# Stick-breaking attention in chunks of at most 512 keys, as one continuous pipeline, with the kept fractions left in PSUM

## The chip, the cores and the metric

The kernel runs on one core of a Trainium2 chip. The metric is the device time of one execution in microseconds. The profile names the engines PE (TensorE, matrix products; PEld is its weight loads), DVE (VectorE), ACT (ScalarE), POOL (GpSimd) and SP (SyncE, which issues most DMAs). Each engine works through its own instructions in a fixed order and waits at an instruction whose inputs or buffers are not ready.

## The reference

One decoder layer on 1024 tokens of 1024 channels. After a first norm and an input projection, two attention families run side by side (NSA, and stick-breaking); they are projected up, merged by gates, projected out, and a squared-ReLU channel mixer follows. The change touches stick-breaking attention alone: 8 heads of 64 channels, strictly causal, with a running product over keys in place of a softmax.

```python
z = jnp.einsum('bqhd,bshd->bhqs', qb, k).astype(jnp.float32) * scale
mask = key_pos[None, :] < t[:, None]
log_keep = jnp.where(mask, jax.nn.log_sigmoid(-z), 0.0)
suffix = lax.cumsum(log_keep, axis=3, reverse=True) - log_keep
a = jnp.where(mask, jnp.exp(jax.nn.log_sigmoid(z) + suffix), 0.0)
return jnp.einsum('bhqs,bshd->bqhd', a.astype(v.dtype), v)
```

So the weight of key s for query t is sigmoid(z) at s times the product of sigmoid(-z), the kept fractions, over all keys between s and t.

## The kernel before

The kernel takes its stages one after another: norm and projections, NSA attention, stick-breaking attention, up projections and merge, output projection, channel mixer. While the two attention stages run, a side stream of matrix products fills TensorE: `fill_all` computes 28 column blocks of the input projection, 48 products of 512 columns each (line 739, tiles `pd`). `drive` (lines 1027 to 1036) steps through the attention's generator; each step yields a nominal cost, and `drive` then issues fill products until their nominal 0.216 us each have used up `cost * ratio + extra`. For stick-breaking the ratio is 0.6 and the extra 0.1, and the last 96 products are kept back for the time after the stage.

A head's queries and keys are loaded from a DRAM buffer and split into a high and a low part (`prep`: a cast on ScalarE, three instructions on GpSimd); values are turned and split for two heads at a time (`prep_v`). The stage then takes 16 families, the lower four row tiles (`g` = 0, rows 0 to 3 of 128 queries) and the upper four (`g` = 1, rows 4 to 7) of each head.

`sb_a` does the first half of a family. Row tile i has n = 128 (i + 1) keys. Its scores come in one PSUM bank (tile `psx`, three buffers), or in two when n is over 512, by products with Kh and Kl and one that adds the causal mask (lines 1109 to 1112). ScalarE turns each bank into the kept fractions, `keep` in SBUF, and into `sig` in SBUF (lines 1113, 1114). One score bank later, `fin` runs for the whole row of n keys: VectorE scans `keep` from its last key to its first into the running product `Pt` (line 1122; its second input is a broadcast zero, in SBUF too), and GpSimd multiplies `sig` by it (line 1124).

`sb_b` does the second half, one family later, interleaved with the next `sb_a`. Key tile n goes upwards from 0: up to four 128x128 pieces of `sig` are transposed into one bank `pt` (line 1140, two buffers); ScalarE casts it to `th`, VectorE subtracts for `tl` (lines 1153, 1154, three buffers each); two products with the values add them to the one bank `po` (line 1145). When the last key tile is in, ScalarE copies half of the bank out (line 1161), VectorE adds the other half (`osum`, line 1163), and SP stores the sum. The next family's first product into `po` must wait for that read.

All instructions of one engine stand in the order of a planner; a dependency set by `behind` keeps fill products behind the attention products they were traced after.

Of the kernel before, what the change touches and what calls it, by code (L numbers as in the profile page):

```python
# [6 lines left out]
F32 = mybir.dt.float32  # L7
# [8 lines left out]
S = 1024  # L16
# [19 lines left out]
def build(tc, I, out):  # L36
# [31 lines left out]
    def rsqrt(dst, ssum, n, tmp):  # L68
        """dst = (ssum / n + eps) ** -0.5, one Newton step behind the table's root; tmp: two more tiles"""
# [36 lines left out]
    # ---------------------------------------------------------------- constants  # L106
# [23 lines left out]
    # ---------------------------------------------------------------- x and the modulation  # L130
    def mod_cols():
# [11 lines left out]
        # (1 + b) g of the first scale  # L143
# [94 lines left out]
    def split_w1(raw, n, m=0):  # L238
        """columns of one contraction tile; the last m of them in tiles of their own"""
# [13 lines left out]
    # query rows: norm, gain and 1/8, then transposed to DRAM  # L253
# [23 lines left out]
    # with the contraction outermost: both compression inputs (transposed) and three tiles of queries  # L277
# [36 lines left out]
    # the first half of the tokens goes ahead for two contraction tiles  # L314
# [92 lines left out]
    # later modulation rows (gate1, shift2, scale2, gate2): partial sums, kept for the end  # L407
# [47 lines left out]
    # relative-position bias: one row per distance, then Toeplitz tiles through DRAM  # L455
# [12 lines left out]
    def bias_cmp():  # L468
# [4 lines left out]
        # row 127 - p holds what distance 128 + p - x asks for; the exchange matrix turns the rows round  # L473
# [11 lines left out]
    # compressed blocks: two positions of one head to a contraction  # L485
# [14 lines left out]
    def compress(which):  # L500
# [9 lines left out]
        def add(g, hs=(0, 1)):  # L510
            # rows r * 64 + d, block c, pair of positions j: src[d, 16 c + 8 g + 2 j + r] + pos[8 g + 2 j + r, d]
# [65 lines left out]
    # selected and window keys and values, and the branch gates  # L577
# [65 lines left out]
    done = [("q", t, qb[t]) for t in range(3)]   # products that wait for their elementwise part  # L643
    turn = []                                   # those that wait for their transposes
# [51 lines left out]
    # column blocks of the input projection, transposed: out[cols, t]  # L696
# [23 lines left out]
    def track(ins):  # L720
        """the attention's latest instruction on the tensor engine"""
        last[:] = [ins.ins]

    def behind(ins):
        """the filling products keep behind the attention's instructions they were traced after"""
# [24 lines left out]
    # ---------------------------------------------------------------- NSA attention  # L750
# [10 lines left out]
    # and the strictly causal one of a diagonal block  # L761
# [36 lines left out]
    # scores, row maxima and exponentials of two heads; the weights end up scaled by gate over sum  # L798
    def nsa_a(i, kv, hp, qT, P):
# [41 lines left out]
        # compressed blocks  # L841
# [15 lines left out]
        # the chunks of a row share its maximum  # L857
# [21 lines left out]
    # transposed weights times values: rows 0-63 of the result carry V's high part, 64-127 its low part  # L879
# [76 lines left out]
    def interleave(ga, na, gb, nb_, lead):  # L956
        """steps of ga with steps of gb spread over those after the first `lead`"""
# [69 lines left out]
    def drive(main, fill, ratio, extra=0.0, keep=0):  # L1027
        """fill beside the main work, all but the last `keep` products of it"""
# [9 lines left out]
    def pump(fill, us):  # L1038
        """that much of it without waiting for anything"""
# [8 lines left out]
    # ---------------------------------------------------------------- stick-breaking attention  # L1048
    def sb_gens(sp):
# [14 lines left out]
        def prep(h, ld):  # L1064
            """split the head's operands, one engine instruction or two per step"""
# [31 lines left out]
        def sb_a(g, ops, A):  # L1097
            Q, Kh, Kl = ops
            late = []
            for i in range(4 * g, 4 * g + 4):  # L1100
                n = 128 * (i + 1)
                keep = sp.tile([128, S], F32, name="keep", bufs=2)
                sig = sp.tile([128, 512 * (g + 1)], F32, name="sig%d" % g, bufs=4)
                A[i] = sig
                for c0, c1 in ([(0, n)] if n <= 512 else [(n - 512, n), (0, n - 512)]):
                    p = psx()
                    w = c1 - c0
                    qs = Q[:, i * 128:(i + 1) * 128]
                    track(nc.tensor.matmul(p[:, :w], qs, Kh[:, c0:c1], start=True, stop=False))
                    track(nc.tensor.matmul(p[:, :w], qs, Kl[:, c0:c1], start=False, stop=c1 != n))  # L1110
                    if c1 == n:
                        track(nc.tensor.matmul(p[:, w - 128:w], identr, diagr, start=False, stop=True))
                    nc.scalar.activation(keep[:, c0:c1], p[:, :w], AF.Sigmoid, scale=-(HD ** -0.5))  # L1113
                    nc.scalar.activation(sig[:, c0:c1], p[:, :w], AF.Sigmoid, scale=HD ** -0.5)  # L1114
                    if late:
                        late.pop(0)()
# [441 lines left out]
```

## Time and profile before

| | us |
|---|---|
| three timed runs | 1803.51, 1809.74, 1809.12 |
| median | 1809.12 |
| span of the profiled execution | 1806.0 |
| stick-breaking stage in it, from the first transposes of values (631.2) to its last product (901.5) | 270.3 |

The profile is of one execution; its times count from the start of its span. An instruction's row has its start, its duration and its engine. Busy time is the union of an engine's instructions. A matrix product's row is longer than the distance to the next one, because products overlap in the array.

### The profile page before, as it was taken

How to read it: one execution, taken by the hardware profiler on the slowest of the kernel's cores; microseconds unless marked ns; L12 is line 12 of the kernel's file. 1: busy time of each engine (PE TensorE's matmuls, PEld its weight loads, DVE VectorE, ACT ScalarE, POOL GpSimd, SP SyncE). 2: the span in 40 equal slices, each digit the busy share in tenths (PEclk: the TensorE clock that was granted, in tenths of full speed). 3: DMA queues.
4: the chain of work that ended last, by engine and by line, in shares of the span. 5: the costliest groups of instructions: out<-in, count | busy, mean ns of one | idle time of the engine just before them, and what ended most of it. 6: DMA issues, size and time to landing. Idle time of an engine off the chain costs nothing.

```text
span 1806.0 us, 25077 instructions
## 1 busy us (share of the span) xinstructions
PE 1705.9 (94%) x8620; PEld 1418.7 (79%) x8620; DVE 1181.2 (65%) x2459; ACT 784.9 (43%) x1745; POOL 1004.8 (56%) x889
## 2 busy tenths in 40 slices
PE   5888999999999979888799999999999999999998
PEld 4768889888888867677678788688888888888886
DVE  7797578778777486767744466256556565657458
ACT  5423376666666355545532234333333333333332
POOL 5463243444333476745338434487677685868576
PEclk9999999999999999989899999999999999999999
DMA  9355412112111342321086462311111121202012
GB/s 298 86 153 170 114 48 60 53 52 61 46 53 41 110 115 76 97 74 36 24 272 191 153 203 59 116 40 55 47 58 59 35 66 40 70 24 71 25 34 93
DMA packets 151047, 157.15 MB, mean 87 GB/s; under 512 B 13240, under 2 KB 112776, under 8 KB 150920
## 3 DMA queue, kind: packets, MB, share of 16 engines
q1 hardware_dynamic: 146696, 153.45, 28.4%
q10 hardware_dynamic: 4224, 2.10, 0.4%
q8 instruction: 68, 1.11, 0.3%
q14 instruction: 59, 0.48, 0.1%
HBM read 128.24 MB, written 27.28 MB: 86 GB/s over the span
## 4 chain that ended last, share of the span: by engine, by line
PE 73%; DVE 9%; POOL 6%; issue 5%; DMA 4%; ACT 2%; SPq 0%; POOLq 0%; ACTq 0%; DVEq 0%
PE px L1457 20%; PE px L1506 16%; PE pd L739 14%; PE px L1370 5%; PE po L902 4%; PE pt L936 3%; DVE Pt L1122 2%; PE psx L818 2%; PE psx L819 2%; PE po L1145 2%; DMA adraw<-in_ada_w_dram 1%; PE pt L1140 1%; POOL adacc L441 1%; PE cb L298 1%; POOL wh L63 1%
## 5 line engine op out<-in xcount | busy, mean ns | idle before, releaser
L1509 DVE TENSOR_TENSOR acc<-acc,px 128x512 f32<-128x512 f32 x384 | 243.8, 681 | 122.5 <-PE px L1506 116.7
L1457 PE MATMUL px<-mtl,wh 128*128 128x512 f32 x512 | 205.0, 400 | 0.0
L1457 PE MATMUL px<-mth,wh 128*128 128x512 f32 x512 | 202.1, 395 | 0.0
L1457 PE MATMUL px<-mth,wl 128*128 128x512 f32 x512 | 201.2, 393 | 0.0
L739 PE MATMUL pd<-uh,uwh 128*128 128x512 f32 x448 | 183.2, 409 | 0.7 <-ACT zo L1011 0.7
L739 PE MATMUL pd<-ul,uwh 128*128 128x512 f32 x448 | 178.7, 399 | 0.0
L66 DVE TENSOR_TENSOR wl<-raw,wh 128x1024 fp32r<-128x1024 f32 x48 | 74.6, 1553 | 159.1 <-ACT wh L61 133.9
L739 PE MATMUL pd<-uh,uwl 128*128 128x512 f32 x448 | 178.2, 398 | 0.0
L1506 PE MATMUL px<-wbl,rah 128*128 128x512 f32 x448 | 175.7, 392 | 2.1 <-POOL wbl L1482 1.8
L1506 PE MATMUL px<-wbh,ral 128*128 128x512 f32 x448 | 174.7, 390 | 0.0
L1506 PE MATMUL px<-wbh,rah 128*128 128x512 f32 x448 | 172.8, 391 | 0.0
L1482 POOL TENSOR_TENSOR wbl<-raw,wbh 128x1024 fp32r<-128x1024 f32 x40 | 104.0, 2600 | 92.3 <-ACT wbh L1481 92.1
L1124 POOL TENSOR_TENSOR sig<-sig,Pt 128x128 f32<-128x128 f32 (+3 forms) x64 | 100.5, 1578 | 83.0 <-ACT sig L1114 42.8
L894 DVE TENSOR_TENSOR tl<-pt,th 128x512 fp32r<-128x512 f32 (+8 forms) x168 | 103.6, 619 | 34.2 <-ACT th L893 33.4
L1480 POOL TENSOR_TENSOR raw<-r 128x512 f32<-128x512 f32 x80 | 109.9, 1394 | 21.1 <-DVE wl L66 19.0
L1122 DVE TENSOR_TENSOR_SCAN Pt<-keep,zero 128x128 f32<-128x128 f32 (+3 forms) x64 | 109.3, 1726 | 13.9 <-ACT keep L1113 3.7
L1457 PEld LDWEIGHTS px<-mth,wh 128*128 128x128 f32 x512 | 96.3, 188 | 24.5 <-issue 0.2
L893 ACT CAST th<-pt 128x512 fp32r<-128x512 f32 (+8 forms) x168 | 88.6, 530 | 61.4 <-PE pt L936 58.8
L1457 PEld LDWEIGHTS px<-mth,wl 128*128 128x128 f32 x512 | 96.3, 188 | 23.8 <-issue 0.8
L1457 PEld LDWEIGHTS px<-mtl,wh 128*128 128x128 f32 x512 | 96.4, 188 | 22.8 <-DVE ral L1489 0.5
L1481 ACT CAST rah<-raw 128x1024 fp32r<-128x1024 f32 x40 | 42.0, 1050 | 153.8 <-PE px L1506 140.5
L875 POOL TENSOR_TENSOR pcx<-pcx,tot 128x64 f32<-128x64 f32 (+7 forms) x32 | 10.5, 330 | 172.0 <-DVE tot L873 82.6
(326 smaller groups left out, 4706.4 us busy)
## 6 DMA issues: line engine op xcount, KB each, us to landing
adraw<-in_ada_w_dram SPq DMA_DIRECT2D x64, 256.0 KB, 2.9
raw<-in_mlp_w_dram SPq DMA_DIRECT2D x32, 512.0 KB, 4.2
w<-in_mlp_w_dram SPq DMA_DIRECT2D x32, 512.0 KB, 3.5
z_d<-zo SPq DMA_DIRECT2D x56, 256.0 KB, 2.1
uwr<-in_w_in_dram SPq DMA_DIRECT2D x54, 256.0 KB, 3.1
xa<-in_ada_w_dram SPq DMA_DIRECT2D x32, 256.0 KB, 5.8
zr<-z_d SPq DMA_DIRECT2D x32, 256.0 KB, 4.0
m<-z_d SPq DMA_DIRECT2D x32, 256.0 KB, 3.6
```

Of the source, the lines that this page charges most:

```text
L66: (nc.vector if e == "v" else nc.gpsimd).tensor_tensor(dst, src, f(h), op=OP.subtract)
L739: r = nc.tensor.matmul(p, a, b, start=(k == 0 and n == 0), stop=(k == NK - 1 and n == 2))
L893: nc.scalar.copy(th[:rows, :w], p[:rows, :w])
L894: nc.vector.tensor_tensor(tl[:rows, :w], p[:rows, :w], f(th)[:rows, :w], op=OP.subtract)
L1122: nc.vector.tensor_tensor_scan(Pt[:, 0:n][:, ::-1], keep[:, 0:n][:, ::-1], zero.to_broadcast([128, n]), 1.0, op0=OP.mult, op1=OP.add)
L1124: nc.gpsimd.tensor_tensor(sig[:, :n], sig[:, :n], Pt[:, 1:n + 1], op=OP.mult)
L1370: nc.tensor.matmul(p, a[:, k, ts_], b[:, k % 2], start=(k == 0 and n == 0), stop=(k == NK - 1 and n == 2))
L1457: nc.tensor.matmul(p, a[:, k], b[th][:, k], start=(k == 0 and m == 0), stop=(k == NK - 1 and m == 2))
L1480: nc.gpsimd.tensor_tensor(d, block(i0, j0, s), block(i1, j1, s), op=OP.add if sg > 0 else OP.subtract)
L1482: (nc.vector if e == "v" else nc.gpsimd).tensor_tensor(l.rearrange("p s n -> p (s n)"), src, f(h).rearrange("p s n -> p (s n)"), op=OP.sub ...
L1506: nc.tensor.matmul(p, a[:, s, qs], b[:, s], start=(s == 0 and n == 0), stop=(s == 1 and n == 2))
L1509: nc.vector.tensor_tensor(acc[:, t, ds_], acc[:, t, ds_], p, op=OP.add if sg > 0 else OP.subtract)
```

## The change

Only `sb_a`, `sb_b` and `sb_all` are rewritten, and one call of `drive`; the rest of the diff removes comments and is left out here.

- The work of a head is now in three kinds of groups of four chunks each. Kind 0: rows 3 to 0, all their keys. Kind 1: rows 7 to 4, the last 512 keys of each. Kind 2: rows 7 to 4, the keys before these (512, 384, 256, 128). The chunks have the widths that the score banks had before, but each chunk now has a scan and a multiplication of its own: 96 scans for 64. A chunk of kind 2 starts its scan from the last value of the row's chunk of kind 1, which a one-column copy on VectorE brings next to it.
- The kept fractions are written by ScalarE back into the score bank (`p`, in PSUM), after `sig` and not before it, and the scan reads them there. The tile `keep` is gone. The bank is held until the scan is done.
- Rows and key tiles go downwards. One step does one chunk's scores and sigmoids, the scan and multiplication of the chunk before, the transposes of one key tile of the group before, the products with values of tiles split earlier, and the split of the tile turned a step before. `bank`, `turned` and `split_` carry tiles over from family to family.
- A family's first products with values are put off by one step (`wait`). Its first product covers only the columns of one row tile; the rest of the bank is written by later ones.
- `th` and `tl` have four buffers, `Pt` six of 513 columns, `sig` five or two.
- The ratio of `drive` is 0.55 and its extra 0.08.

```diff
-        def sb_a(g, ops, A):
...
-                    nc.scalar.activation(keep[:, c0:c1], p[:, :w], AF.Sigmoid, scale=-(HD ** -0.5))
-                    nc.scalar.activation(sig[:, c0:c1], p[:, :w], AF.Sigmoid, scale=HD ** -0.5)
...
-                    nc.vector.memset(Pt[:, n:n + 1], 1.0)
-                    nc.vector.tensor_tensor_scan(Pt[:, 0:n][:, ::-1], keep[:, 0:n][:, ::-1],
-                                                 zero.to_broadcast([128, n]), 1.0, op0=OP.mult, op1=OP.add)
-                    nc.gpsimd.tensor_tensor(sig[:, :n], sig[:, :n], Pt[:, 1:n + 1], op=OP.mult)
...
+        def chunks_of(kind):
+            rows = range(3, -1, -1) if kind == 0 else range(7, 3, -1)
+            out_ = []
+            for i in rows:
+                n = 128 * (i + 1)
+                out_.append((i,) + ((0, n), (n - 512, n), (0, n - 512))[kind])
+            return out_
+
+        def sb_a(kind, chunk, ops, A, edges):
...
+            sig = sp.tile([128, w], F32, name="sigr" if kind == 1 else "sig%d" % w, bufs=5 if kind == 1 else 2)
+            nc.scalar.activation(sig, p[:, :w], AF.Sigmoid, scale=HD ** -0.5)
+            nc.scalar.activation(p[:, :w], p[:, :w], AF.Sigmoid, scale=-(HD ** -0.5))
+            A[i, kind] = (sig, c0)
+
+            def fin():
+                Pt = sp.tile([128, 513], F32, name="Pt", bufs=6)
+                if diag:
+                    nc.vector.memset(Pt[:, w:w + 1], 1.0)
+                else:
+                    nc.vector.tensor_copy(Pt[:, w:w + 1], edges.pop(i)[:, 0:1])
+                nc.vector.tensor_tensor_scan(Pt[:, 0:w][:, ::-1], p[:, 0:w][:, ::-1], zero.to_broadcast([128, w]),
+                                             1.0 if diag else Pt[:, w:w + 1], op0=OP.mult, op1=OP.add)
+                nc.gpsimd.tensor_tensor(sig, sig, Pt[:, 1:w + 1], op=OP.mult)
+                if kind == 1:
+                    edges[i] = Pt
...
+                for c in range(4):
+                    cost = 0.0
+                    if k < len(groups):
+                        fin, cost = sb_a(kind, chunks[c], ops[h], A[h, min(kind, 1)], edges)
+                        late.append(fin)
+                        yield cost
+                    if len(late) > 1 or k == len(groups):
+                        if late:
+                            late.pop(0)()
+                    cost = 0.0
+                    if k > 0:
+                        hb, kb = groups[k - 1]
+                        g = min(kb, 1)
+                        cost += turn(hb, g, (3, 7, 3)[kb] - c, A[hb, g])
+
+                        if split_ and (wait[0] or split_[0][2] != 4 * split_[0][1] + 3):
+                            while len(split_) > 0:
+                                cost += times_v(V)
+                            wait[0] = 0
+                        elif split_:
+                            wait[0] = 1
+                        if len(turned) > 1:
+                            halves()
+                    yield cost
...
-    drive(sb_gens(sp), fill, 0.6, 0.1, TAIL)
+    drive(sb_gens(sp), fill, 0.55, 0.08, TAIL)
```

`turn` holds the transposes of one key tile, `halves` the cast and the subtraction, `times_v` the two products with values and, after key tile 0, the read of the bank; each is the old code of `sb_b` with its tiles taken from the lists.

## Rows read from the trace of the kernel before

**Rows 1.** The page: span, and busy time, share of the span and instructions of each engine.

```profile
span 1806.0 us, 25077 instructions
PE 1705.9 (94%) x8620; PEld 1418.7 (79%) x8620; DVE 1181.2 (65%) x2459; ACT 784.9 (43%) x1745; POOL 1004.8 (56%) x889
```

**Rows 2.** Busy time by stretch: the whole stage, the part of it in which fill products run, the last whole piece of that part, and the part without them. Columns: from and to, length, busy time and instructions of PE, PEld, DVE, ACT and POOL, granted clock, DMA share, GB/s.

```profile
631.20:901.50 270.30, 229.43 (x1173) 188.09 (x1172) 195.26 (x279) 147.36 (x336) 161.98 (x103) 0.92 0.26 71
...
631.20:866.30 235.10, 203.79 (x1048) 168.08 (x1047) 170.91 (x244) 128.82 (x297) 151.57 (x96) 0.95 0.29 79
...
832.00:866.30 34.30, 31.66 (x171) 26.48 (x170) 24.99 (x41) 18.70 (x45) 17.95 (x14) 1.00 0.10 32
866.30:901.50 35.20, 25.64 (x126) 20.01 (x125) 24.35 (x36) 18.54 (x40) 10.42 (x7) 0.76 0.07 19
```

**Rows 3.** Timeline of PE in a piece without a wait: start, duration, instruction, and how many stand together.

```profile
847.27 0.39 PE L739 MATMUL pd<-uh,uwh 128*128 128x512 f32 x1
847.50 0.39 PE L1145 MATMUL po<-th,V 128*128 128x512 f32 x1
...
848.43 0.60 PE L1140 MATMUL pt<-ident,sig 128*128 128x128 f32 x4
848.78 0.48 PE L1145 MATMUL po<-tl,V 128*128 128x512 f32 x1
849.10 0.39 PE L739 MATMUL pd<-ul,uwh 128*128 128x512 f32 x1
```

**Rows 4.** Groups of instructions on PE in the stage, 631.2 to 901.5 (one of three groups of fill products, the transposes, one of two groups of products with values, one of two of scores): count, then busy time and mean ns, then idle time before them and its releasers.

```profile
L739 PE MATMUL pd<-uh,uwh 128*128 128x512 f32 x135 | 57.1, 423 | 0.0
L1140 PE MATMUL pt<-ident,sig 128*128 128x128 f32 x288 | 53.3, 295 | 25.7 <-DVE tl L1154 14.5 <-DVE V L1092 5.5 <-POOL sig L1124 3.5
L1145 PE MATMUL po<-tl,V 128*128 128x512 f32 (+1 forms) x96 | 41.3, 431 | 6.2 <-DVE tl L1154 6.2
...
L1109 PE MATMUL psx<-Kh,Q 128*128 128x512 f32 (+2 forms) x96 | 34.7, 365 | 1.3 <-ACT sig L1114 1.3
```

**Rows 5.** The same groups in the last whole piece with fill products (832 to 866.3; one of three), and the line of the fill products from 631.2 to 866.3 with the first and last start of this group.

```profile
L739 PE MATMUL pd<-uh,uwh 128*128 128x512 f32 x24 | 9.7, 403 | 0.0
...
L739 PE MATMUL pd<-uh,uwl x135: 387/393/628, 631.8 to 865.8; 128*128 128x512 f32 x135
```

**Rows 6.** Who waited for whom, the weight loads of PE in the stage: us in total, times, longest.

```profile
PEld pt L1140 <- DVE tl L1154: 20.0, 17, 4.3
PEld po L1145 <- DVE tl L1154: 7.1, 5, 2.4
PEld pt L1140 <- POOL sig L1124: 5.9, 4, 2.0
PEld po L1145 <- DVE osum L1163: 5.6, 7, 1.9
...
PEld psx L1109 <- ACT sig L1114: 1.5, 1, 1.5
```

**Rows 7.** Timeline of DVE: four scans, 128 columns twice, 512 and 1024 once, and a low part of a fill weight, both of whose inputs lie in SBUF.

```profile
658.36 2.56 DVE L1122 TENSOR_TENSOR_SCAN Pt<-keep,zero 128x128 f32<-128x128 f32 x1 [1.29 <-ACT sig L1114]
...
675.01 0.69 DVE L66 TENSOR_TENSOR uwl<-uwr,uwh 128x512 fp32r<-128x512 f32 x1
...
790.60 2.27 DVE L1122 TENSOR_TENSOR_SCAN Pt<-keep,zero 128x1024 f32<-128x1024 f32 x1
...
836.29 1.21 DVE L1122 TENSOR_TENSOR_SCAN Pt<-keep,zero 128x512 f32<-128x512 f32 x1
...
860.63 0.40 DVE L1122 TENSOR_TENSOR_SCAN Pt<-keep,zero 128x128 f32<-128x128 f32 x1
```

**Rows 8.** Timeline of POOL: the low part of a head's keys, and multiplications of 128 and 512 columns.

```profile
658.28 2.35 POOL L66 TENSOR_TENSOR Kl<-zr,Kh 128x1024 fp32r<-128x1024 f32 x1
...
763.35 0.41 POOL L1124 TENSOR_TENSOR sig<-sig,Pt 128x128 f32<-128x128 f32 x1
...
867.20 1.09 POOL L1124 TENSOR_TENSOR sig<-sig,Pt 128x512 f32<-128x512 f32 x1 [1.25 <-DVE Pt L1122]
```

**Rows 9.** The lines of the scan and of the subtraction `tl` in the stage: count, then minimum, median and maximum duration in ns.

```profile
L1122 DVE TENSOR_TENSOR_SCAN Pt<-keep,zero x64: 401/1694/3833, 635.4 to 885.4; 128x128 f32<-128x128 f32 x8, 128x256 f32<-128x256 f32 x8, 128x384 f32<-128x384 f32 x8, 128x512 f32<-128x512 f32 x8
...
L1154 DVE TENSOR_TENSOR tl<-pt,th x96: 258/608/693, 650.1 to 901.0; 128x512 fp32r<-128x512 f32 x48, 128x384 fp32r<-128x384 f32 x16, 128x256 fp32r<-128x256 f32 x16, 128x128 fp32r<-128x128 f32 x16
```

**Rows 10.** Groups of instructions of DVE and POOL in the stage, columns as in the groups of PE.

```profile
L1122 DVE TENSOR_TENSOR_SCAN Pt<-keep,zero 128x128 f32<-128x128 f32 (+3 forms) x64 | 109.3, 1726 | 13.9 <-ACT keep L1113 3.7 <-issue 3.6 <-ACT sig L1114 2.9
L1154 DVE TENSOR_TENSOR tl<-pt,th 128x512 fp32r<-128x512 f32 (+1 forms) x96 | 51.4, 546 | 37.1 <-ACT th L1153 35.0 <-ACT sig L1114 1.6
L66 DVE TENSOR_TENSOR uwl<-uwr,uwh 128x512 fp32r<-128x512 f32 x18 | 20.1, 1139 | 4.6 <-POOL uwh L63 4.6
...
L1121 DVE MEMSET Pt<- 128x1 f32 x62 | 3.7, 59 | 7.9 <-POOL sig L1124 7.0 <-PE pt L1140 0.8
...
L1124 POOL TENSOR_TENSOR sig<-sig,Pt 128x128 f32<-128x128 f32 (+3 forms) x64 | 100.5, 1578 | 83.0 <-ACT sig L1114 42.8 <-DVE Pt L1122 19.2 <-DVE Pt L1121 13.6
```

**Rows 11.** Groups of instructions of ACT in the stage: kept fractions, `sig` and the cast `th`.

```profile
L1113 ACT ACTIVATE keep<-psx 128x512 f32<-128x512 f32 (+2 forms) x96 | 47.9, 508 | 50.6 <-DVE Pt L1122 24.8 <-PE psx L1112 10.2 <-DVE Pt L1121 8.1
L1114 ACT ACTIVATE sig<-psx 128x512 f32<-128x512 f32 (+2 forms) x96 | 47.7, 511 | 18.9 <-PE pt L1140 17.9 <-POOL Q L1073 0.7
L1153 ACT CAST th<-pt 128x512 fp32r<-128x512 f32 (+1 forms) x96 | 46.7, 492 | 34.4 <-PE pt L1140 33.7
```

More of the change, by code (lines that the diff above doesn't have):

```diff
@@ new lines, in sb_gens, with turn @@
+        bank, turned, split_, wait = {}, [], [], [0]
+        def turn(h, g, kt, A):
+            p = pt()
+            c0 = max(0, kt - 4 * g) * 128
+            for i in range(max(4 * g, kt), 4 * g + 4):
+                o = (i - 4 * g) * 128
+                sig, s0 = [A[i, x] for x in ((0,) if g == 0 else (1, 2)) if (i, x) in A and
+                           A[i, x][1] <= kt * 128 < A[i, x][1] + A[i, x][0].shape[1]][0]
+                track(nc.tensor.transpose(p[:, o:o + 128], sig[:, kt * 128 - s0:kt * 128 - s0 + 128], ident))
+            turned.append((h, g, kt, c0, p))
+            return (512 - c0) / 128. * PT_
@@ new lines, in sb_all @@
+            groups = [(h, kind) for h in range(8) for kind in range(3)]
+            A, edges, late = {}, {}, []
+            extra = []
+            for k in range(len(groups) + 1):
+                if k < len(groups):
+                    h, kind = groups[k]
+                    if kind == 0:
+                        A[h, 0] = {}
+                        if h + 1 < 8:
+                            lds[h + 1] = (load((h + 1) // 2, h + 1), load(4 + (h + 1) // 2, h + 1))
+                            if h % 2 == 1:
+                                vr = load_v((h + 1) // 2)
+                    if kind == 1:
+                        A[h, 1] = {}
+                        if h + 1 < 8:
+                            extra.append(prep(h + 1, lds[h + 1]))
+                            if h % 2 == 1:
+                                extra.append(prep_v(vr, V))
+                    chunks = chunks_of(kind)
+                for c in range(4):
+                    cost = 0.0
+                    if k < len(groups):
+                        fin, cost = sb_a(kind, chunks[c], ops[h], A[h, min(kind, 1)], edges)
[18 more added lines that the diff above has]
+                    yield cost
+                    for e in list(extra):
+                        r = next(e, "end")
+                        if r == "end":
+                            extra.remove(e)
+                        elif isinstance(r, tuple):
+                            ops[h + 1] = r
+                        elif r:
+                            yield r
+                if k < len(groups) and kind == 2:
@@ L1205, in sb_all @@
                                 ops[h + 1] = r
-                    prev = (h, g, V[h], A)
-            for c in sb_b(*prev):
-                yield c
+                            elif r:
+                                yield r
+                    extra = []
+            while turned or split_:
+                cost = 0.0
+                while split_:
+                    cost += times_v(V)
+                if turned:
+                    halves()
+                yield cost
         return sb_all()
```

118 lines of the change are left out of this document (33 added, 85 removed).

## The prediction

> **What bounds the kernel now.** I read the page first [rows 1]: TensorE is busy for 94% of the span, so only stretches in which it has holes can give anything back. The change touches one stage, so I cut that stage out by time [rows 2]: it runs from 631.2 to 901.5, 270.3 us, and here TensorE is busy for 229.4 us, VectorE for 195.3, GpSimd for 162.0 and ScalarE for 147.4. No engine is full. The reader should also see the granted clock: 1.00 in the piece from 832 to 866.3, 0.92 over the stage, 0.76 in the last piece. Where TensorE has holes its clock falls between its two levels, 1.2 and 2.4 GHz, and that costs time again.
>
> Busy time flatters TensorE, since its rows overlap, so I counted its work by distances between starts [rows 3]. A product of 512 columns takes 0.23 us (847.27 to 847.50). Four transposes and one such product take 0.67 (848.43 to 849.10), so a transpose takes (0.67 - 0.23) / 4 = 0.11. A mask product of 128 columns I count as a quarter of 0.23, 0.06. The stage has [rows 4] 3 x 135 = 405 fill products (93.2 us); scores and products with values of 8 heads, 18432 columns a head or 36 x 0.23 (66.2); 64 masks (3.7); 288 transposes of weights and 32 of values (35.2). That is 198.3 us, 73% of the stage; 72 us are holes and slow clock. The 768 instructions that are no fill take 105.1 us, 0.137 each.
>
> Where are the 72 us? The last fill product before the end starts at 865.8 [rows 5]. Behind it 126 instructions [rows 2], 17.3 us of work, take 35.2: 49%, 17.9 us lost. Ahead of it 181.0 us of work take 235.1: 77%, 54.1 us lost. The best piece, 832 to 866.3, has 3 x 24 fill products [rows 5] and 99 others, 16.6 + 13.6 = 30.1 us in 34.3: 88%. The waits name what TensorE's weight loads stand for [rows 6]: `tl` with 20.0 and 7.1 us, the multiplied `sig` with 5.9, the read of the one bank `po` with 5.6. So the stage is bound by what VectorE and GpSimd hand back late, and at its end by a lack of fill.
>
> Why is `tl` late? Its own length isn't the reason, 693 ns at most [rows 9]. It stands in VectorE's queue behind scans, and these are long: 401 ns at least, 3833 at most. A scan of 128 columns takes 0.40 us once and 2.56 another time [rows 7]; the long one starts at 658.36 and ends at 660.92, and beside it GpSimd works from 658.28 to 660.63 [rows 8]. The scan stood for the whole of that instruction. Both of its inputs lie in SBUF. `tl`, which has one of its two in PSUM, never stretches.
>
> **The change part by part.**
>
> *The scan reads PSUM.* Undisturbed scans take 0.40, 1.21 and 2.27 us for 128, 512 and 1024 columns [rows 7], 2.09 ns a column, so the eight lengths of a head take 10.7 us and the stage 85.6. They took 109.3 [rows 10]: 23.7 us, 0.37 a scan, are waits for GpSimd. After, a head has six scans of 512 and two each of 384, 256 and 128: 7.26 + 2 x (0.94 + 0.67 + 0.40) = 11.28 us, the stage 90.2. I take it that a scan with one input in PSUM waits for GpSimd as little as `tl` does. Then VectorE has 195.3 - 109.3 + 90.2 = 176.2 us. Multiplications gain likewise: 0.41 and 1.09 us for 128 and 512 columns alone [rows 8], or 0.18 + 1.77 ns a column, give 82.6 us for the 96 against 100.5 now [rows 10]; GpSimd goes to 144.
>
> What does a PSUM input cost by itself? `tl` of 512 columns takes up to 0.69 us with one input in PSUM [rows 9]; a subtraction of the same size with both in SBUF takes 0.69 alone [rows 7]. So nothing, and the sum goes by that. A rule speaks against it: the Trainium skill, Perfetto Trace Analysis, section Optimizing Scalar/DVE Operations, gives VectorE about 60 ns of access time on SBUF and about 125 on PSUM. By it 96 scans would cost some 6 us more on VectorE (an estimate from that page), and the forecast would be 1774 at most; the rows show no such difference.
>
> *The copies.* 32 one-column copies: 0.059 each if they are like the one-column memset [rows 10], 1.9 us; at most 1.09 each, if each waits for a multiplication of 512 [rows 8], 35 us. I take 1.9, since the memset is the nearest in size; VectorE has 178 us.
>
> *ScalarE writes into PSUM.* No row of before shows that. The kept fractions take 47.9 us now [rows 11]. If reading and writing one bank took turns they would take twice that, and ScalarE 195 us in place of 147; if it is cheaper than SBUF, the gain falls on an engine that is idle for 45% of the stage. I take 0, as `sig` and the kept fractions, same reads, cost the same; the upper end stays in the range.
>
> *The bank is held for the scan.* Cost on the path: none with three banks, since one chunk's products, two sigmoids and scan take 0.5 + 1.0 + 1.2 us [rows 3, 7, 11] against three steps of 228.6 / 96 = 2.4. Behind a score product that waits stand all transposes, products with values and fill. What if that cover fails is a rival below.
>
> *Downwards, a step at a time.* Each transposed piece is now multiplied three steps ahead of its use, for row 7 as for row 4. The waits for `sig` (5.9) and, through `wait`, for `po` (5.6) go; the longest instruction ahead of a `tl` in VectorE's queue is 1.2 us, no longer 2.3 to 3.8. What is late next is `tl` itself, behind ScalarE's `sig`, kept fractions and `th` of the same step. `th`, `tl`, loads, head splits and stores are as many as before; they cost nothing new. The fourth buffers and the reversed accumulation cost nothing either.
>
> *The fill.* By the code the generator yields 250 times before, 132.3 us of nominal cost; (132.3 x 0.6 + 250 x 0.1) / 0.216 = 483 products wanted, and 404 are to be had (the trace has 405). They run out at yield 211. After, the same cost comes in 208 yields: (132.3 x 0.55 + 208 x 0.08) / 0.216 = 414. So the fill lasts to nearly the end; the 96 kept for the time after stay.
>
> *The sum.* The last four steps, 16 transposes and 8 products with values, have no fill: 3.6 us of work at 49%, 7.3 us. The other 194.7 us I take at the level of the best piece of before, 88%: 221.3. The stage takes 228.6 in place of 270.3, 41.7 less: 14 from the end without fill, 27.5 from the rest. VectorE would then be busy for 178 / 228.6 = 78%, against 73% in the best piece [rows 2]; that is why I take no more than 88%. The profiled execution's span goes from 1806.0 to 1764.3. It is 3.1 us shorter than the median of the runs, 1809.1, so the forecast is 1767.4.
>
> **The rivals.**
>
> *A: the scan still waits for GpSimd* (the change doesn't do what it says): its broadcast zero, and in kind 2 its start value, still come from SBUF. Then 96 scans wait 0.37 us each, 35.5 us on VectorE. Of the waits of TensorE listed above about half stand behind `tl`, so I put half of it on the path: stage 246.4, time 1785. Against: `tl` has an SBUF input too. The Trainium skill says, in SBUF — State Buffer, section Who interferes with whom, that a VectorE instruction with at most one SBUF input outside the two-port modes doesn't contend with GpSimd; by that rule A is out for kinds 0 and 1, and of a start value it says nothing there.
>
> *B: the pace is not made by the scans.* If the in-order coupling of four engines keeps the part with fill at 77%, only the end gains: 194.7 / 0.77 + 7.3 = 260.2, time 1799. For it: without its best piece the part with fill comes to 150.9 us of work in 200.8, 75%, with the same code.
>
> *C, slower: the chain of a step closes on itself.* A chunk's bank is free only after its scan; `th` waits behind the next chunk's two sigmoids, `tl` behind a scan, the transposes two steps on behind `tl`. If these run one behind the other, a head takes 4.6 (scores) + 11.95 (sigmoids) + 11.28 (scans) + 5.84 (`th`) + 6.43 (`tl`) = 40.1 us, eight heads 321, 51 more than now: 1860. It decides from the point at which neighbouring steps hide less than 16% of that chain. For it: shared buffers are few (three banks, two of `pt`), and kept fractions now come after `sig`. Against: score products wait for banks for only 1.5 us in the stage now [rows 6].
>
> **How the numbers follow.** Forecast 0.55, A 0.14, B 0.16, C 0.15. With the pace between 82% and 94% the forecast's own range is 1753 to 1784; the upper ends of the copies and of ScalarE's writes reach to A's time. The range of 1748 to 1805 takes in A and B and leaves C out with a little below. Half a per cent, 9 us, is what a measurement can tell here. Forecast and A are faster, B lies on the edge (half faster, most of the rest same), and C's milder part, if steps hide just about 16%, is no change: faster 0.77, same 0.10, slower 0.13.
>
> **What would show it.** Scans of 512 columns at 1.2 us each, their sum near 90, none over 2, multiplications near 83: the lock is gone; if not, A. TensorE's waits for `osum` and `sig` gone, those for `tl` under 15 us. The last fill product within 10 us of the stage's end. A stage of 229 us with a granted clock above 0.95. Sigmoids into PSUM at 0.6 us for 512 columns. Score products that wait for a scan by more than 20 us in all would show C, and a stage above 270 makes the forecast wrong; a stage near 260 with short scans would say that the scans never set the pace.

## The result, and the profile after

Four runs of the changed kernel have a median of 1764.22 us (1761.23 to 1768.14), four of the kernel before 1808.65 (1803.51 to 1809.74). The ratio is 0.977, with a 95% interval of 0.974 to 0.979: faster by 2.3%. The forecast was 1767.4 us.

The page of the changed kernel, span and engines, beside [rows 1]:

```profile
span 1759.5 us, 25142 instructions
PE 1689.0 (96%) x8620; PEld 1407.6 (80%) x8620; DVE 1163.7 (66%) x2523; ACT 784.9 (45%) x1745; POOL 977.7 (56%) x921
```

The profiled execution is 46.5 us shorter. Busy time by stretch, beside [rows 2]: the stage, the part with fill products, the part without. Columns as there.

```profile
632.30:857.80 225.50, 212.93 (x1173) 176.63 (x1172) 175.50 (x340) 147.27 (x336) 135.84 (x135) 1.00 0.32 86
632.30:852.60 220.30, 208.86 (x1152) 173.93 (x1151) 171.92 (x335) 144.92 (x332) 134.80 (x134) 1.00 0.33 87
852.60:857.80 5.20, 4.07 (x22) 2.71 (x21) 3.58 (x5) 2.35 (x4) 1.04 (x2) 1.00 0.13 50
```

The stage takes 225.5 us where it took 270.3, 44.8 less. Its first instruction is 1.1 us later and what follows it takes 2.8 us less, so the rest of the program hardly moves. TensorE does the same 1173 products at a granted clock of 1.00, not 0.92. VectorE has 20 us less to do with 61 instructions more, GpSimd 26 less with 32 more, ScalarE the same. Without fill stand 22 instructions and 5.2 us at the end, where there were 126 and 35.2.

Groups of the stage on VectorE, GpSimd and ScalarE, beside [rows 10, 11], columns as there.

```profile
L1131 DVE TENSOR_TENSOR_SCAN Pt<-psx,zero 128x512 f32<-128x512 f32 (+1 forms) x64 | 64.5, 1019 | 18.0 <-ACT psx L1122 16.0 <-ACT sigr L1121 1.2
L1157 DVE TENSOR_TENSOR tl<-pt,th 128x128 fp32r<-128x128 f32 (+2 forms) x96 | 51.7, 541 | 15.0 <-ACT th L1156 14.6
L1133 POOL TENSOR_TENSOR sig<-sig,Pt 128x512 f32<-128x512 f32 (+1 forms) x64 | 48.0, 765 | 34.1 <-DVE Pt L1131 31.0 <-DVE Pt L1128 1.7 <-PE po L1168 1.0
L1122 ACT ACTIVATE psx<-psx 128x512 f32<-128x512 f32 (+1 forms) x96 | 47.8, 498 | 0.0
...
L1133 POOL TENSOR_TENSOR sigr<-sigr,Pt 128x512 f32<-128x512 f32 x32 | 36.8, 1154 | 31.1 <-DVE Pt L1131 30.4 <-DVE Pt L1130 0.4
...
L1131 DVE TENSOR_TENSOR_SCAN Pt<-psx,Pt,zero 128x512 f32<-128x512 f32 (+3 forms) x32 | 27.9, 878 | 5.1 <-ACT psx L1122 4.7
...
L66 DVE TENSOR_TENSOR uwl<-uwr,uwh 128x512 fp32r<-128x512 f32 x18 | 17.8, 1000 | 2.1 <-POOL uwh L63 2.1
...
L1130 DVE COPY Pt<-Pt 128x1 f32<-128x1 f32 x32 | 4.6, 143 | 0.7
```

The reader is to see the scans: 64.5 + 27.9 = 92.4 us in 96 instructions, where 64 took 109.3. Multiplications take 48.0 + 36.8 = 84.8 us, where they took 100.5. `tl` and the sigmoids cost what they did; the copies take 143 ns each.

The line of the scan, beside [rows 9], shows that nothing stretches any more: minimum, median and maximum in ns.

```profile
L1131 DVE TENSOR_TENSOR_SCAN Pt<-psx,zero x64: 415/1211/1225, 637.2 to 832.5; 128x512 f32<-128x512 f32 x40, 128x384 f32<-128x384 f32 x8, 128x256 f32<-128x256 f32 x8, 128x128 f32<-128x128 f32 x8
L1131 DVE TENSOR_TENSOR_SCAN Pt<-psx,Pt,zero x32: 468/880/1280, 649.6 to 841.6; 128x512 f32<-128x512 f32 x8, 128x384 f32<-128x384 f32 x8, 128x256 f32<-128x256 f32 x8, 128x128 f32<-128x128 f32 x8
```

It can be seen happening. Timeline of VectorE (start, duration), then of GpSimd at the same time:

```profile
654.42 1.22 DVE L1131 TENSOR_TENSOR_SCAN Pt<-psx,zero 128x512 f32<-128x512 f32 x1 [0.23 <-ACT psx L1122]
...
658.41 0.42 DVE L1131 TENSOR_TENSOR_SCAN Pt<-psx,zero 128x128 f32<-128x128 f32 x1
```

```profile
654.85 2.39 POOL L66 TENSOR_TENSOR Kl<-zr,Kh 128x1024 fp32r<-128x1024 f32 x1
657.32 2.40 POOL L1073 TENSOR_TENSOR Q<-zr,Q 64x1024 fp32r<-64x1024 f32 x1
```

Beside the low part of a head's keys a 128-column scan took 2.56 us before [rows 7, 8]; now such a low part begins in the middle of a 512-column scan, which still takes 1.22 us. The scan of 128 columns at 658.41 takes 0.42 and ends at 658.83, 0.89 us ahead of the instruction on the queries that GpSimd began before it.

Last, who waited for whom in the stage, beside [rows 6]: us, times, longest.

```profile
PEld psx L1116 <- DVE Pt L1131: 11.8, 14, 1.6
PE psx L1116 <- DVE Pt L1131: 7.7, 11, 1.3
...
PE pt L1148 <- DVE tl L1157: 2.1, 3, 0.9
...
PEld pt L1148 <- DVE tl L1157: 1.7, 2, 0.9
...
PEld po L1168 <- DVE osum L1174: 0.7, 2, 0.4
PEld pt L1148 <- POOL sig L1133: 0.6, 1, 0.6
```

The transposes' waits for `tl` go from 20.0 us to 1.7 on weight loads (14.5 [rows 4] to 2.1 on the products themselves), those for `osum` and `sig` from 5.6 and 5.9 to under 1. A new one stands at the head: a score product's weight load waits 11.8 us in all for a scan to give back its PSUM bank. (Loads and products are two views of one stall; their times are not added.)

### The profile page after: what moved, and what is told of

It reads as the page before. It is cut to its first block, busy times and chain, and to the rows that moved or that the text cites. A ratio compares the mean times of both kernels' runs of the same rounds, so it can differ in the third digit from the quotient of the medians.

```text
span 1759.5 us, 25142 instructions
## 1 busy us (share of the span) xinstructions
PE 1689.0 (96%) x8620; PEld 1407.6 (80%) x8620; DVE 1163.7 (66%) x2523; ACT 784.9 (45%) x1745; POOL 977.7 (56%) x921
## 4 chain that ended last, share of the span: by engine, by line
PE 72%; DMA 8%; POOL 8%; DVE 6%; issue 3%; ACT 2%; SPq 0%; POOLq 0%; DVEq 0%; ACTq 0%
PE px L1501 20%; PE px L1550 16%; PE pd L739 15%; DMA adraw<-in_ada_w_dram 5%; PE po L902 4%; PE pt L936 4%; POOL adacc L441 2%; PE psx L818 2%; PE psx L819 2%; PE po L1168 2%; PE pt L1148 1%; POOL adraw L439 1%; DVE Pt L1131 1%; PE cb L298 1%; DMA m<-z_d 1%
## 5 line engine op out<-in xcount | busy, mean ns | idle before, releaser
L1526 POOL TENSOR_TENSOR wbl<-raw,wbh 128x1024 fp32r<-128x1024 f32 x40 | 104.5, 2614 | 92.4 <-ACT wbh L1525 92.2
L893 ACT CAST th<-pt 128x512 fp32r<-128x512 f32 (+8 forms) x168 | 88.7, 531 | 61.1 <-PE pt L936 58.5
L875 POOL TENSOR_TENSOR pcx<-pcx,tot 128x64 f32<-128x64 f32 (+7 forms) x32 | 10.5, 329 | 172.0 <-DVE tot L873 82.6
L1550 PEld LDWEIGHTS px<-wbl,rah 128*128 128x128 f32 x448 | 84.0, 188 | 21.4 <-POOL wbl L1526 3.1
L1550 PEld LDWEIGHTS px<-wbh,rah 128*128 128x128 f32 x448 | 84.0, 188 | 19.1
```

The source lines that it names most:

```text
L893: nc.scalar.copy(th[:rows, :w], p[:rows, :w])
L1526: (nc.vector if e == "v" else nc.gpsimd).tensor_tensor(l.rearrange("p s n -> p (s n)"), src, f(h).rearrange("p s n -> p (s n)"), op=OP.sub ...
L1550: nc.tensor.matmul(p, a[:, s, qs], b[:, s], start=(s == 0 and n == 0), stop=(s == 1 and n == 2))
```

## Experiments

The theory of the prediction: a scan with both inputs in SBUF waits for GpSimd, and reading PSUM removes that wait; it is the main cause, and fill and order add the end. The rivals: the order itself, the shorter scans, or the longer fill. Each ratio below is to the kernel before, with its 95% interval, from runs on the same chip. A stage's length is that of one profiled execution: the change's is 225.5 us above and 227.2 in e11, so a difference of 2 us between two stages says nothing.

### Taking PSUM away from the change

**e3_new_keep_sbuf.** The new order, with the kept fractions in SBUF:

```diff
-            nc.scalar.activation(p[:, :w], p[:, :w], AF.Sigmoid, scale=-(HD ** -0.5))
+            keep = sp.tile([128, 512], F32, name="keep", bufs=3)
+            nc.scalar.activation(keep[:, :w], p[:, :w], AF.Sigmoid, scale=-(HD ** -0.5))
...
-                nc.vector.tensor_tensor_scan(Pt[:, 0:w][:, ::-1], p[:, 0:w][:, ::-1], zero.to_broadcast([128, w]),
+                nc.vector.tensor_tensor_scan(Pt[:, 0:w][:, ::-1], keep[:, 0:w][:, ::-1], zero.to_broadcast([128, w]),
```

> The changed kernel with the kept fractions in a tile of SBUF (three buffers) in place of the score bank, so that both inputs of a scan lie in SBUF and the bank is free after the sigmoids. Theory 1: scans stretch again, 96 x 0.37 = 35 us more on VectorE, half of it on the path, 1780 to 1785. Theory 2: within half a per cent of 1764. If holding the bank costs more than the waits for GpSimd, faster than 1764.

Measured: 1788.55 us, 0.992 (0.989 to 0.994); of the change's 2.3% only 0.8% is left, and the loss is a bit more than theory 1 says (1780 to 1785). Groups of scans in its stage and the writing of `keep`, then the stage by busy time, then two waits:

```profile
L1132 DVE TENSOR_TENSOR_SCAN Pt<-keep,zero 128x512 f32<-128x512 f32 (+1 forms) x64 | 84.8, 1355 | 7.7 <-ACT keep L1123 7.6
...
L1123 ACT ACTIVATE keep<-psx 128x512 f32<-128x512 f32 (+1 forms) x96 | 45.4, 512 | 5.4 <-DVE Pt L1132 3.3 <-DVE Pt L1131 1.7 <-DVE Pt L1129 0.3
...
L1132 DVE TENSOR_TENSOR_SCAN Pt<-keep,Pt,zero 128x512 f32<-128x512 f32 (+3 forms) x32 | 38.3, 1232 | 0.9 <-ACT keep L1123 0.9
```

```profile
632.90:884.30 251.40, 219.33 (x1173) 181.59 (x1172) 209.40 (x339) 145.96 (x336) 167.69 (x135) 0.97 0.29 77
```

```profile
PE pt L1149 <- DVE tl L1158: 18.9, 17, 6.5
...
PEld pt L1149 <- POOL sig L1134: 7.5, 5, 3.3
```

The same 96 scans take 84.8 + 38.3 = 123.1 us, 30.7 more than the change's 92.4, or 0.32 each. GpSimd has 167.7 us, 32 more: the two delay each other. The wait for `tl` is back at once (`PE`, 18.9 us in 17 waits, 2.1 in the change), and so is that for `sig` (7.5 us): the new order alone takes neither away. The stage is 25.9 us longer, though the bank is now free before the scan and ScalarE hardly waits for a buffer of `keep` (3.3 us). So the place of one operand is worth over half of the stage's gain, with order, chunks and fill as they are in the change.

**e4_new_keep_sbuf_hold.** The same, but with the bank held until the scan is done, by a one-column read behind it:

```diff
+                hold = sp.tile([128, 1], F32, name="hold", bufs=2)
+                nc.vector.tensor_tensor(hold, p[:, 0:1], Pt[:, 0:1], op=OP.add)
```

> The changed kernel with the kept fractions in SBUF, as in the run that took 0.992 of the time before, and with a one-column read of the score bank behind every scan on VectorE, which holds the bank as long as the change does and costs 96 x 0.14 = 13 us on VectorE. The added one-column result is used by nothing. If holding the bank is cheap (my sum: nothing), 1784 to 1795; if the hold itself costs as much as the waits for GpSimd do, 1800 or more.

Measured: 1802.33 us, 0.997 (0.996 to 0.999); stage 264.1 us, 12.7 more than in e3. That lies in the range named for a dear hold, but the 96 reads take 13.8 us of VectorE themselves (145 ns each), and products and transposes wait for the same instruction. So the price of the hold can't be told from that of the reads; this run says only that both together cost 12.7 us where the scans are slow already.

### Giving PSUM and short scans to the kernel before

**e5_old_psum_chunks.** The old order and its fill; the scan goes bank by bank, reads PSUM, and starts from the value of the bank before:

```diff
-                    nc.scalar.activation(keep[:, c0:c1], p[:, :w], AF.Sigmoid, scale=-(HD ** -0.5))
                     nc.scalar.activation(sig[:, c0:c1], p[:, :w], AF.Sigmoid, scale=HD ** -0.5)
+                    nc.scalar.activation(p[:, :w], p[:, :w], AF.Sigmoid, scale=-(HD ** -0.5))
...
+                        nc.vector.tensor_tensor_scan(Pt[:, c0:c1][:, ::-1], p[:, 0:w][:, ::-1], zero.to_broadcast([128, w]),
+                                                     1.0 if c1 == n else Pt[:, c1:c1 + 1], op0=OP.mult, op1=OP.add)
+                        nc.gpsimd.tensor_tensor(sig[:, c0:c1], sig[:, c0:c1], Pt[:, c0 + 1:c1 + 1], op=OP.mult)
```

> The kernel before, old order and old fill, with one thing of the change: every score bank has a scan and a multiplication of its own, at most 512 keys, and the scan reads the kept fractions in the bank. Theory 1: scans as short as in the changed kernel, 92 us in all, and 20 to 27 us off the time, 1782 to 1789. Theory 2: under 9 us, 1800 or more.

Measured: 1770.76 us, 0.982 (0.980 to 0.984), 11 us below the range of theory 1. Its scans, then its stage, part with fill and part without, then two waits:

```profile
L1122 DVE TENSOR_TENSOR_SCAN Pt<-psx,zero 128x512 f32<-128x512 f32 (+2 forms) x64 | 64.8, 1016 | 17.0 <-ACT psx L1113 15.9 <-issue 0.9
...
L1122 DVE TENSOR_TENSOR_SCAN Pt<-psx,Pt,zero 128x128 f32<-128x128 f32 (+3 forms) x32 | 28.2, 880 | 4.0 <-ACT psx L1113 2.4
```

```profile
633.80:865.90 232.10, 217.57 (x1174) 178.70 (x1173) 172.73 (x311) 147.07 (x336) 136.09 (x135) 0.99 0.30 84
633.80:835.90 202.10, 194.16 (x1048) 161.58 (x1047) 150.69 (x275) 128.40 (x296) 126.61 (x125) 0.99 0.33 93
835.90:865.90 30.00, 23.42 (x127) 17.12 (x127) 22.03 (x36) 18.68 (x40) 9.48 (x11) 0.94 0.09 23
```

```profile
PEld pt L1141 <- DVE tl L1155: 6.3, 9, 2.7
...
PEld pt L1141 <- POOL sig L1124: 2.2, 1, 2.2
```

The scans cost what they cost in the change, 93.0 us. The stage is 38 us shorter than before, of the change's 45, in the old order. The part with fill does its 181 us of work in 202.1, 90%, where it was 77%. The waits for `tl` and `sig`, 20.0 and 5.9 us before, are down to 6.3 and 2.2 without the new order.

**e6_old_sbuf_chunks.** The same without PSUM: scans bank by bank, kept fractions in SBUF and ahead of `sig` as before.

```diff
+                        nc.vector.tensor_tensor_scan(Pt[:, c0:c1][:, ::-1], keep[:, c0:c1][:, ::-1], zero.to_broadcast([128, w]),
+                                                     1.0 if c1 == n else Pt[:, c1:c1 + 1], op0=OP.mult, op1=OP.add)
```

> The kernel before, old order and old fill, with scans and multiplications of at most 512 keys each, but the kept fractions still in SBUF. It tells the length of the scans from where they read. Theory 1 in its strict form (waits for GpSimd are the cost): 96 scans wait in place of 64, no gain, 1805 to 1815. If the length ahead of a subtraction in VectorE's queue is the cost: 10 to 20 us off, 1789 to 1799.

Measured: 1798.30 us, 0.997 (0.996 to 0.999): some gain, at the slow end of the second range, where the strict form of theory 1 has none. Its scans and the writing of `keep`, then its stage:

```profile
L1123 DVE TENSOR_TENSOR_SCAN Pt<-keep,zero 128x512 f32<-128x512 f32 (+2 forms) x64 | 87.7, 1379 | 16.5 <-issue 9.0 <-ACT keep L1113 3.7 <-ACT th L1155 2.0
...
L1113 ACT ACTIVATE keep<-psx 128x512 f32<-128x512 f32 (+2 forms) x96 | 48.0, 508 | 51.1 <-PE psx L1112 16.7 <-DVE Pt L1123 15.6 <-DVE Pt L1122 13.7
...
L1123 DVE TENSOR_TENSOR_SCAN Pt<-keep,Pt,zero 128x128 f32<-128x128 f32 (+3 forms) x32 | 37.1, 1158 | 1.5 <-ACT keep L1113 0.5
```

```profile
633.40:896.40 263.00, 228.70 (x1174) 187.94 (x1173) 204.18 (x311) 147.53 (x336) 172.08 (x135) 0.94 0.27 74
```

They take 124.8 us, more than the 109.3 of the 64 long ones. The stage is 7 us shorter all the same; that shorter scans let other work in between is the likely reason, not a shown one. But they wait oftener: (124.8 - 93.0) / 96 = 0.33 us each, beside the same scans in e5. Before it was 0.37 each for 64. So in these two kernels cutting the scans up didn't make the wait of one shorter; as GpSimd's multiplications went from 64 to 96 with them, it isn't shown what sets its length. Of what was tried, only the change of place takes it away. e5 differs from e6 in one more thing than place and the sigmoids' order: in e6 ScalarE stands 15.6 us behind scans before it can write `keep`, which has two buffers here. e3, with three, shows the loss without that.

### The fill

**e1_old_fill055.** The kernel before with the new fill rate alone.

```diff
-    drive(sb_gens(sp), fill, 0.6, 0.1, TAIL)
+    drive(sb_gens(sp), fill, 0.55, 0.08, TAIL)
```

> The kernel before with nothing but the fill's ratio 0.55 and extra 0.08. Theory 1 (scans that wait for GpSimd and are long set the pace; the end without fill is a cost of its own, 14 us): the fill lasts to within some 15 us of the stage's end and the time falls by 10 to 14 us, to about 1796. Theory 2 (the new order makes the gain) says no change, 1806 to 1810, because the holes that the fill leaves at the front come back there. Theory 3 (the fill's ratio is most of the gain): 1780 or less.

Measured: 1800.36 us, 0.997 (0.996 to 0.999): 5 us less than the kernel before on the same chip (1805.42), at most half of what theory 1 said. Its stage, part with fill and part without, then its scans:

```profile
633.60:895.80 262.20, 225.01 (x1174) 185.59 (x1173) 197.38 (x280) 147.12 (x336) 164.55 (x103) 0.94 0.27 74
633.60:884.80 251.20, 215.52 (x1120) 178.78 (x1118) 188.90 (x266) 141.27 (x324) 161.74 (x101) 0.94 0.27 75
884.80:895.80 11.00, 9.49 (x54) 6.81 (x55) 8.48 (x16) 5.85 (x12) 2.81 (x3) 1.00 0.18 48
```

```profile
L1122 DVE TENSOR_TENSOR_SCAN Pt<-keep,zero 128x128 f32<-128x128 f32 (+3 forms) x64 | 116.0, 1825 | 15.3 <-issue 7.6 <-ACT keep L1113 6.2 <-ACT otmp L1161 0.8
```

The part without fill shrinks from 35.2 us to 11.0, but the stage only from 270.3 to 262.2. The fill that the end gets is missing in the part ahead of it, which takes 251.2 us in place of 235.1. The scans take 116.0 us, 6.7 more than before, though nothing about them was changed: (116.0 - 85.6) / 64 = 0.48 us of waiting each, with the prediction's 85.6 for undisturbed ones.

**e10_old_psum_fill055.** e5 with the same edit.

> The old order with a scan for every score bank that reads the bank (the kernel that took 0.982 of the time before), and with the fill's ratio 0.55 and extra 0.08 as well. What it still lacks of the change is the order alone: downwards, one step at a time, the put-off first product. Theory 1 (scans in PSUM, then the fill): 1762 to 1767, no more than half a per cent from the changed kernel's 1764. Theory 2 (the order has a share of its own of 8 us or more): 1771 or more, that is no gain from the fill in the old order.

Measured: 1771.53 us, 0.980 (0.978 to 0.982): the same as e5, and in the range of theory 2. Stage and part with fill:

```profile
634.90:868.80 233.90, 220.08 (x1174) 182.46 (x1173) 172.40 (x311) 147.32 (x336) 135.11 (x135) 0.96 0.31 83
634.90:856.20 221.30, 209.46 (x1120) 174.30 (x1118) 163.89 (x297) 141.56 (x324) 133.37 (x133) 0.97 0.32 85
```

The end is short (13 us), the stage is not: 233.9 against 232.1. The part with fill does (405 fill products at 0.23 and 715 others at 0.137) 191 us of work in 221.3, 86% where e5 had 90%.

**e2_new_fill060.** The changed kernel with the old fill rate (the same line, the other way).

> The changed kernel with the old ratio 0.6 and extra 0.1. By the yields 193 products more than half of the pace are wanted early, the fill runs out some 15% before the stage's end. Theory 1 as predicted: without fill the pace is VectorE's, and about 11 us are lost, 1775. If the end without fill costs little once scans don't wait for GpSimd: 1764 to 1769.

Measured: 1772.51 us, 0.981 (0.979 to 0.983), between the two theories. Stage and part without fill:

```profile
632.90:865.30 232.40, 217.88 (x1173) 179.46 (x1172) 176.84 (x339) 147.16 (x336) 134.68 (x135) 0.99 0.31 83
...
845.60:865.30 19.70, 16.07 (x85) 11.76 (x84) 15.41 (x25) 11.29 (x25) 5.32 (x8) 0.91 0.10 28
```

So the new order with the old fill is e5 again, and the old order with the new fill is e5 again (0.980 to 0.982); only both together reach 0.977 to 0.978. That step is small: the intervals of e10 and e2 overlap with the change's.

### What else is in the order

**e7_new_no_put_off.** The change without its one-step delay of a family's first products with values:

```diff
-                        if split_ and (wait[0] or split_[0][2] != 4 * split_[0][1] + 3):
+                        if split_:
```

> The changed kernel without the put-off: a family's first product with values comes one step earlier, right behind the last family's end. By my account the waits for the read of the one bank, 5.6 us before, come back, in part hidden: 1766 to 1770. If the put-off matters to the order as a whole: 1772 or more; if the step in between covers the read anyway: no change, 1762 to 1767.

**e11_change_again.** The change as it is, on the chip of e7, e12 and e13.

> The changed kernel as it is, on the chip and beside the runs of the three below. 0.977 of the time before, 1763 to 1768.

Measured: 1767.42 us for e7, 0.978 (0.976 to 0.980); 1767.12 for e11, 0.978 (0.976 to 0.980). The time is level with that of e11 and the waits for `osum` do not come back (1.1 us on weight loads, 0.7 in e11): the delay does nothing that can be measured.

### A shorter chain on ScalarE

**e9_new_difference.** The running product at a key is the one behind it times the kept fraction, so its drop from the one to the other is the weight. That needs no `sig` on ScalarE:

```diff
-            nc.scalar.activation(sig, p[:, :w], AF.Sigmoid, scale=HD ** -0.5)
...
-                nc.gpsimd.tensor_tensor(sig, sig, Pt[:, 1:w + 1], op=OP.mult)
+                nc.gpsimd.tensor_tensor(sig, Pt[:, 1:w + 1], Pt[:, 0:w], op=OP.subtract)
```

> The changed kernel without the second sigmoid: the weight of a key is the running product behind it less the one with it, P(s+1) - P(s), so GpSimd subtracts two columns of Pt where it multiplied, and ScalarE does 96 sigmoids in place of 192, 48 us less work. The rounding differs from the product's. If the stage is now bound by TensorE's own work (198 of 226 us) with holes that stand behind score banks held for two sigmoids and a scan: those holes, 8 to 13 us, go, 1752 to 1757. If ScalarE hides entirely: 1760 to 1766.

Measured: 1759.72 us, 0.974 (0.972 to 0.975); stage 221.6 us. It falls between the two ranges, nearer to the second: of the 8 to 13 us of the first it gets about 4. ScalarE goes from 147 us to 111, and the score products' wait for the bank, where no second sigmoid stands ahead of the scan any more, shrinks:

```profile
PEld psx L1116 <- DVE Pt L1130: 7.9, 14, 1.2
PE psx L1116 <- DVE Pt L1130: 3.9, 10, 0.7
```

**e12_new_difference_again.** The same kernel beside the change, five runs each.

> The kernel that takes the weight as a difference of running products, with more rounds, to tell it from the changed kernel. If the stage that is 4 us shorter in its profile carries over: 0.973 to 0.975 of the time before and clear of the changed kernel; if not, intervals that overlap widely.

Measured: 1760.63 us (1758.46 to 1765.06), 0.974 (0.972 to 0.976), beside 1767.12 (1765.47 to 1769.22) of e11. No run of the one reaches the other.

**e13_old_psum_difference.** The same edit in e5, so with the old order and the old fill.

> The old order and the old fill, with a scan for every score bank that reads the bank, and the weight as a difference of running products (one sigmoid a bank). If the new order is needed for what the change gains beyond the scans: 1766 to 1771, as without the difference or slightly better; if a shorter chain on ScalarE does the same as the order: 1758 to 1764.

Measured: 1759.18 us (1756.96 to 1760.84), 0.973 (0.971 to 0.975), the best time here, level with e12. With one sigmoid a bank the old order and fill lose nothing beside the new ones. Both e12 and e13 beat both kernels. The score products' loads wait 1.3 us for a scan in e13, 10.8 in e5. Whether the bank that comes free sooner or ScalarE's lighter work makes the gain, these runs don't separate.

## Why the prediction was right

**The scan reads PSUM: right, and the main cause, shown.** Predicted 90.2 us of scans, measured 92.4; multiplications 82.6 and 84.8; VectorE 178 and 175.5; GpSimd 144 and 135.8, lower since its other instructions in the stage (`Kl`, `Q`, `Kh`, `uwh`) took 62.7 us before and take 52.3 now. e3 against the change and e5 against e6 are the same swap in two orders: 25.9 and 30.9 us of stage (263.0 - 232.1; e5 also turns the two sigmoids round and has no `keep` to wait for). Rival A is out, its start value included: no scan is over 1280 ns. Had A held, its price was too low: it put half of the extra scan time on the path, since "about half" of TensorE's waits stood behind `tl`. By the rows it names it was 27.1 us of 38.6, 70% [rows 6], and in e3 the stage lost 25.9 us for 30.7 of scans, 84%.

**PSUM input costs nothing: right.** 512 columns take 1.22 us, from SBUF 1.21 [rows 7].

**The copies: mis-sized.** 143 ns each, not 59: 4.6 us in place of 1.9. **The bank held for the scan: mis-sized.** It was put at nothing, on the ground that three banks cover a chunk's 2.7 us; the weight loads of scores wait 11.8 us, the largest wait that is left. The cover fails in part because a scan has to wait for the second sigmoid (16.0 us in the group of scans) and for its turn on VectorE, which the 2.7 us leave out. One case of the second, from the timeline of all engines:

```profile
702.49 0.86 DVE L66 TENSOR_TENSOR uwl<-uwr,uwh 128x512 fp32r<-128x512 f32 x1
...
703.27 1.27 DVE L1131 TENSOR_TENSOR_SCAN Pt<-psx,Pt,zero 128x512 f32<-128x512 f32 x1
...
704.59 0.19 PEld L1116 LDWEIGHTS psx<-Kh,Q 128*128 128x128 f32 x1 [1.61 <-DVE Pt L1131]
```

A fill weight is ahead of the scan, and the weight load that waits for the scan stands for 1.61 us. e9, without the second sigmoid, brings the 11.8 us to 7.9. That is the first link of rival C, at under the 20 us that were named as its sign; the rest of C's chain didn't close. What the hold costs by itself stays open: e4 mixes it with other work, and e9 and e13 lighten ScalarE too.

**ScalarE writes into PSUM: right.** 47.8 us for the kept fractions, 47.9 before [rows 11].

**The fill and the end: right in size by place, wrong by cause.** Of the 44.8 us, 15.7 come from the end by the prediction's own count (3.0 us of work for 22 instructions in 5.2, a loss of 2.2 where it was 17.9) and 29.1 from the part with fill (195.3 us of work in 220.3, 88.7%, a loss of 25.0 where it was 54.1). Predicted were 14, 27.5 and 88%. But these are places, not causes. The short scans alone, in the old order with the old fill (e5), take 38.2 us off the stage, not 27.5 at most; order and fill together add 6.6, not 14. One term was too small and the other too large; that the sum came out so near is in part luck. e1 moved the fill to the end and got 8 us of stage; e10 did it on top of e5 and got nothing; e2 left 20 us of end open and lost 7. A fill product that goes to the end is missing ahead of it; that it is worth something there only if the steps ahead can do without it fits these runs, and nothing tried it by itself. The granted clock of the part with fill was 0.95 before and 0.94 in e1, 0.99 in e5 and 0.97 in e10, and 1.00 in the change; whether the clock or the holes themselves take the gain back was not tried apart. The 88% was read off the best piece of before and not worked out; the same scans give 90% in e5 and 86% in e10.

**Downwards, a step at a time: right on the waits, wrong on its worth.** Those for `sig`, `po` and `tl` are gone as forecast. But in e5, in the old order, most of them are gone as well, and in e3, in the new order, those for `sig` and `tl` are back, so these were late because of the scans. The prediction put the end of the waits for `po` down to `wait`; they stay away without it too (e7). Order and fill together are worth a ratio of 0.977 to 0.978 (the change, e11) against 0.982 (e5), about the half per cent that a measurement can tell, and with one sigmoid a bank nothing (e12 and e13).

**Rival B, that the scans don't make the pace**, is out by e5: the same order with short scans does 90% in the part with fill. **The sum** came out 3.1 us high for the stage: 7.3 us without fill against 5.2, and 221.3 with it against 220.3.

## What to carry to other kernels

Look at the spread of one instruction's durations at one size: where some take several times the shortest, see in the timeline which engine worked beside them. Cutting such an instruction up can cost its engine more, not less (124.8 us of scans for 109.3 here). Where ScalarE's result goes to VectorE only once, leaving it in its PSUM bank can take VectorE off GpSimd's way for no instruction at all; price the bank that is held, with the wait for the reader's turn in it. Filler work moved to a bare end was paid for here, in part or whole, where it was taken from, so first make the steps able to do without it.

## What the hardware showed that was not expected

- The wait of a scan for GpSimd didn't shrink with the scan: on average 0.37 us for each of 64 scans of up to 1024 columns, 0.33 for each of 96 of up to 512 (e6), 0.32 in e3, and nothing that shows with one input in PSUM. It is no constant: another fill rate alone made it 0.48 (e1). What has both inputs in SBUF still pays: the low part of a fill weight takes 1000 ns on average in the changed kernel (`uwl` in the groups), 0.69 us alone [rows 7]. The Trainium skill, SBUF — State Buffer, section Who interferes with whom, says that a VectorE instruction with at most one SBUF input, outside the two-port modes, doesn't contend with GpSimd; the scans agree (512 columns from PSUM: 1.225 us at most), and those whose start value comes from SBUF, of which it says nothing, don't stretch either (1.280 us at most).
- That start value costs some 0.06 us a scan. Groups of scans by shape in the changed kernel, without and with it:

```profile
L1131 DVE TENSOR_TENSOR_SCAN Pt<-psx,zero 128x512 f32<-128x512 f32 x40 | 48.7, 1218 | 9.7 <-ACT psx L1122 9.6
...
L1131 DVE TENSOR_TENSOR_SCAN Pt<-psx,Pt,zero 128x512 f32<-128x512 f32 x8 | 10.2, 1275 | 0.0
L1131 DVE TENSOR_TENSOR_SCAN Pt<-psx,Pt,zero 128x384 f32<-128x384 f32 x8 | 8.1, 1016 | 0.2
...
L1131 DVE TENSOR_TENSOR_SCAN Pt<-psx,zero 128x384 f32<-128x384 f32 x8 | 7.6, 954 | 0.6
```

- A copy of one column takes 143 ns and a sum of two single columns 145 (e4), where a memset of one column takes 59. The prediction's copies were priced by the memset and cost 2.4 times that.
